# First stage of a transformer layer: its sixteen feature blocks in groups of 3, 4, 4 and 5 in place of 4, 4, 4 and 4

## The chip, the core and the metric

The kernel runs on one core of a Trainium2 chip. Its time is the device time of one execution in microseconds; the time before is the median of three runs. TensorE (PE) multiplies and transposes, VectorE (DVE) and ScalarE (ACT) work on elements, GpSimd (POOL) and SyncE (SP) mostly issue DMA transfers. The clock that TensorE was granted was 0.998 of full speed in the profiled execution.

## The reference

One layer: a first gated feed-forward network, a token mixer, a second gated feed-forward network, each with residual and layer norm. The first stage is all that matters here:

```python
ada = jax.nn.silu(c) @ w_ada + b_ada              # w_ada 2048 x 9*2048
sh1, sc1, g1, sh2, ... = jnp.split(ada, 9)
h = layernorm(x) * (1 + sc1) + sh1                # x: 256 x 2048
gate, up = jnp.split(h @ ffn1_w_in, 2)            # ffn1_w_in 2048 x 2*5632
h = (jax.nn.silu(gate) * up) @ ffn1_w_out
```

All is float32. The 2048 features are 16 blocks of 128. Before TensorE can multiply a block of h, that block's shift and scale must be there, and those are sums over all 2048 rows of two columns of w_ada: 16 rows of 128, each scaled by silu(c) and added on DVE (two operations in one instruction), then transposed by TensorE (which puts features on partitions) and reduced by DVE over the 128 partial sums.

## The kernel before, in words

*Products.* Each product of two float32 matrices is three matmuls of rounded parts: `mm3` multiplies high by high, high by low and low by high (L396, L397, L398). So each weight tile that lands from memory (`raw`) is split: ACT casts it to `hi` (L145), DVE subtracts to get `lo` (L146). The same is done with the activations: `modulate_both` normalises four blocks (L316), transposes them on TensorE (L322), applies shift and scale into the one buffer `xf`, copies it to xhi (ACT, L330) and subtracts to xlo (DVE, L332).

*Passes and tiles.* The first 12 of the column strips of ffn1_w_in (24 chunks of gate and up columns, 6144 columns) are worked in four passes, j = 0 to 3, one for each group of four feature blocks, because the shifts and scales of a later group are not there at the start. A pass has 12 tiles, n = 0 to 11: tile n is a weight tile of 512 rows (4 blocks) by 512 columns, one transfer of 1 MB on SP's queue, 48 matmuls (two halves of 24). Results of passes 0 to 2 are added up in `hT` and `gate` by DVE (L836); the last tile of a pass is kept in PSUM and is the first of the next pass. For that the strips rotate by one a pass (`order_of`): in pass 3, tile n holds strip 9, 10, 11, 0, 1, ..., 8. After pass 3 the remaining columns run with all 16 blocks at once.

*The head.* Everything up to the first matmul: `first_ada` brings 16 rows of ada for blocks 0 to 3 (each 128 x 2 x 512, 512 KB, on SP's queue, some in the places of weight tiles), DVE sums them (L158 the first, L160 the others) into `gate`, and the four blocks then go through transposes (L750) and `modulate_both` one after another, woven with the highs and lows of the first weight tile (`raw_first`, four transfers of 256 KB). `load_bcol` brings all nine vectors of biases (144 rows of 128) and transposes them in the head.

*The stream.* `ada_stream` brings the rows of the next three groups, 48 of 512 KB each, on POOL's queue: row r goes into one of three places that rotate (the tag `araw`), and is summed two steps later by DVE. A place is free again when its row is summed, and POOL, which issues its transfers in order, waits for that. How many steps are taken before a tile is written out by hand: a list of 1s and 2s in pass 0, then `1 + ((n - 11) % 3 == 2)` a tile, 16 a pass. In the middle of tile 10 of a pass, `columns0` transposes the finished sums of the next group (L792) and DVE reduces them (L794); then come four blocks of `modulate_both`, which pass j + 1 needs.

*Pass 3* has no stream any more: from its fourth tile on `pump` brings the ada rows of later stages (`ar2_0_...`, also in the three `araw` places, issued by SP), and DVE sums them between the weight tiles' low parts.

*What sets the order.* DVE and ACT of the last piece of the head run in the order that is written; elsewhere a scheduler arranges each engine's instructions from the program order and dependences, and the order is fixed when the kernel is built. Each engine then works strictly in its order. The pair of buffers `h0` (2 x 128 x 512) is not used by the kernel in the first stage; later stages use it.

Of the kernel before, what the change touches and what calls it, by code (L numbers as in the profile page):

```python
# [47 lines left out]
def layer_kernel(  # L48
# [67 lines left out]
    def load_bcol():  # L116
        brow = ap.tile([72, 2, P], F32, tag="acc", name="brow")
        SP.dma_start(brow, b_ada[0].rearrange("(h r p) -> r h p", h=2, p=P))
        bps = aux_tile("bps")
        for i in range(2):  # L120
            PE.transpose(bps[:, i * 72:(i + 1) * 72], brow[:, i, :], ident[:72, :72])
        V.tensor_copy(bcol.rearrange("p v k -> p (v k)"), bps[:, :144])
        for v in (1, 4, 7):
            V.tensor_scalar_add(bcol[:, v, :], bcol[:, v, :], 1.0)
# [4 lines left out]
    def load_mixer_smalls():  # L129
        hrow = ap.tile([6, 1024], F32, tag="acc", name="hrow")  # L130
        SP.dma_start(hrow[0:4, :], mlstm_conv_w[0])
        SP.dma_start(hrow[4:5, :], mlstm_conv_b)
# [8 lines left out]
        V.tensor_copy(hcol.rearrange("p a b -> p (a b)"), hps[:, :48])
# [170 lines left out]
    def modulate_both(v, j, rs, xT):  # L312
        xf = npool.tile([P, 4, T], F32, tag="xf", name=f"xf{ntag()}")
        n = xf.rearrange("p k t -> p (k t)").rearrange("p (a n) -> p a n", a=2)
        for a in range(2):
            S.activation(n[:, a, :], res[:, a, j * 512:(j + 1) * 512], AF.Identity, bias=rs[a][:, 1:2],  # L316
                         scale=rs[a][:, 0:1])
        yield
        tps = [aux_tile(f"tp{ntag()}") for _ in range(2)]
        for q in range(4):  # L320
# [4 lines left out]
        for q in range(4):  # L325
            k = 4 * j + q
# [3 lines left out]
            high[0] = S.copy(hi, xf[:, q, :])  # L330
            yield
            modulated[0] = V.tensor_tensor(out=lo, in0=xf[:, q, :], in1=hi.bitcast(F32), op=ALU.subtract)  # L332
            yield
# [376 lines left out]
    def first_ada(j, ws=iter(())):  # L710
        src = pair_cols(0, j)
        if j % 2:
            acc = ap.tile([P, 2, 512], F32, tag="acc", name=f"acc0_{j}")
        else:
            acc = gate[:, :1024].rearrange("p (v n) -> p v n", v=2)
        for kk in range(8):
            if kk in (2, 5, 7):
                raws = []
                for h in range(2):
                    k = 2 * kk + h  # L720
                    raw = ap.tile([P, 2, 512], F32, tag="araw", bufs=3, name=f"ar0_{j}_{k}")
# [24 lines left out]
        cps += [mm_tile(f"cq{q}") for q in range(3)]
# [13 lines left out]
        for q in range(4):  # L760
            next(mb)
            if q < 3:
                column(q + 1)
            next(mb)
            fence0.append(next(lows))
            if q:
                next(highs, None)
        yield

    def ada_stream():  # L770
        rows = []
        for r in range(3 * KD + 2):
            if r >= 2:
                with behind(modulated[0]):
                    ada_acc(*rows.pop(0))
            if r < 3 * KD:
# [5 lines left out]
                G_.dma_start(raw, pair_cols(0, j)[k * P:(k + 1) * P])  # L782
                rows.append((sums0[j], raw, k))
            yield

    sums0 = {}
# [25 lines left out]
    def first_in(j, n, i, ws, middle=None):  # L812
# [43 lines left out]
    def first_ws():  # L856
        raw = wp.tile([P, 4, 512], F32, tag="raw", bufs=3, name="raw_first")
        for k in range(4):
# [3 lines left out]
        ws.extend((k, *(p[k // 2][:, k % 2, :] for p in parts)) for k in range(4))  # L862
# [13 lines left out]
    fa = first_ada(0, first_ws())  # L876
# [26 lines left out]
    for j in range(4):  # L903
        for n, i in enumerate(order_of(j)):
# [3 lines left out]
            for _ in range((1, 1, 2, 2, 1, 2, 2, 1, 2, 2, 2)[n] if j == 0 and n < 11 else 1 + ((n - 11) % 3 == 2)):  # L908
# [3 lines left out]
            elif n == 7:  # L912
                mb = modulate_both(0, j + 1, rs0, xT)
# [519 lines left out]
    for j in range(2, 10):  # L1433
# [3 lines left out]
        if j == 7:  # L1437
            need(11)
            mb = modulate_both(6, 2, mr2, xT)
# [84 lines left out]
```

## Time and profile before

| | |
|---|---|
| median of three runs | 1920.01 us (1917.58 to 1920.4) |
| profiled execution, device time | 1918.75 us |
| its span in the profile | 1917.1 us |
| TensorE busy | 1871.8 us, 98% of the span |
| DVE, ACT, POOL busy | 76%, 49%, 3% |
| bytes moved | 510.89 MB, mean 266 GB/s |
| length of the first stage's four passes | about the first 300 us |

In rows of one engine's work the first number is the time from the span's start, the second the duration in us, then engine, line, operation, output and inputs, size, and in brackets how long the engine was idle just before and what released it. In the tables of windows each engine has its busy time with the number of instructions. Names of buffers in the profile are cut at their numbers: `s` is any tile's result in PSUM, `ar` any row of ada, `raw_s`, `hi_s`, `lo_s` any weight tile of the passes.

### The profile page before, as it was taken

Reading aid. Unit: us, or ns where it says so; the run is one execution under the profiler, and the core shown is the slowest. Engines: PE = TensorE matmul, PEld = TensorE weight load, DVE = VectorE, ACT = ScalarE, POOL = GpSimd, SP = SyncE. Lnnn points to the kernel's source line nnn. Section 1 sums busy time; section 2 is a strip of 40 time slices with the busy share of each in tenths; the row PEclk is TensorE's granted clock in tenths of the full one; section 3 lists DMA queues with packets and bytes.
Section 4 is the critical chain, followed back from the end, with each engine's and each line's share of the span. In section 5 each row is a group of like instructions: output and inputs, shape, how many; then the busy total and the mean of one; then the engine's idle time right before and its main releaser. Section 6 shows DMA issues by size and latency. Waiting matters only on the chain.

```text
span 1917.1 us, 32186 instructions
## 1 busy us (share of the span) xinstructions
PE 1871.8 (98%) x13101; PEld 1718.4 (90%) x13101; DVE 1463.5 (76%) x1762; ACT 939.7 (49%) x1310; POOL 58.0 (3%) x93
## 2 busy tenths in 40 slices
PE   3999999999999999999999999999999999999997
PEld 3999999999988888698999886999999999988886
DVE  6899879777778899688887887777775654555786
ACT  5554444444454464745655534465444444444562
POOL 1211000000000000000000000000000000000000
PEclk9999999999999999999999999999999999999999
DMA  9999879999889787489888884998687656755562
GB/s 358 371 330 325 287 231 308 327 306 332 286 319 322 264 304 262 154 307 315 274 277 280 310 295 160 322 317 271 230 269 253 218 183 195 241 190 186 196 198 88
DMA packets 295867, 510.89 MB, mean 266 GB/s; under 512 B 10882, under 2 KB 159010, under 8 KB 294696
## 3 DMA queue, kind: packets, MB, share of 16 engines
q1 hardware_dynamic: 287944, 480.53, 73.9%
q0 software_dynamic: 7776, 28.32, 4.0%
q8 instruction: 102, 1.67, 0.4%
q14 instruction: 45, 0.37, 0.1%
HBM read 506.71 MB, written 2.10 MB: 265 GB/s over the span
## 4 chain that ended last, share of the span: by engine, by line
PE 94%; DVE 2%; DMA 1%; ACT 1%; issue 0%; SPq 0%; POOL 0%; DVEq 0%; POOLq 0%
PE o_f L396 8%; PE gu_f L397 8%; PE gu_f L398 8%; PE o_f L398 8%; PE gu_f L396 8%; PE o_f L397 8%; PE s L396 5%; PE s L398 5%; PE s L397 5%; PE fh L398 2%; PE fh L396 2%; PE fh L397 2%; PE fs L396 1%; PE fs L397 1%; PE fs L398 1%; PE o_mx L398 1%
## 5 line engine op out<-in xcount | busy, mean ns | idle before, releaser
L160 DVE SCALAR_TENSOR_TENSOR acc<-ar,csil,acc 128x1024 f32<-128x1024 f32 x240 | 307.5, 1281 | 31.7 <-DMA ar<-in_w_ada_dram 31.0
L397 PE MATMUL gu_f<-xlo_f,hi_f2i 128*128 128x256 f32 x768 | 212.4, 277 | 0.0
L398 PE MATMUL gu_f<-xhi_f,lo_f2i 128*128 128x256 f32 x768 | 212.3, 276 | 0.0
L396 PE MATMUL gu_f<-xhi_f,hi_f2i 128*128 128x256 f32 x768 | 212.3, 276 | 0.0
L396 PE MATMUL s<-xhi_f,hi_s 128*128 128x256 f32 x752 | 208.6, 277 | 0.0
L398 PE MATMUL s<-xhi_f,lo_s 128*128 128x256 f32 x752 | 208.0, 277 | 0.0
L397 PE MATMUL s<-xlo_f,hi_s 128*128 128x256 f32 x752 | 207.9, 277 | 0.0
L146 DVE TENSOR_TENSOR lo_f2i<-raw_f2i,hi_f2i 128x1024 fp32r<-128x1024 f32 x96 | 117.7, 1226 | 102.8 <-ACT hi_f2i L145 102.8
L396 PE MATMUL gu_f<-xhi_f,hi_f1i 128*128 128x256 f32 x640 | 177.1, 277 | 0.0
L398 PE MATMUL gu_f<-xhi_f,lo_f1i 128*128 128x256 f32 x640 | 177.0, 277 | 0.0
L397 PE MATMUL gu_f<-xlo_f,hi_f1i 128*128 128x256 f32 x640 | 176.9, 276 | 0.0
L145 ACT CAST hi_f2i<-raw_f2i 128x1024 fp32r<-128x1024 f32 x96 | 100.8, 1050 | 138.1 <-PE gu_f L397 126.0
L145 ACT CAST hi_s<-raw_s 128x1024 fp32r<-128x1024 f32 x94 | 98.0, 1054 | 111.0 <-PE s L397 82.0
L397 PEld LDWEIGHTS gu_f<-xlo_f,hi_f2i 128*128 128x128 f32 x768 | 144.2, 188 | 0.1
L396 PEld LDWEIGHTS gu_f<-xhi_f,hi_f2i 128*128 128x128 f32 x768 | 144.2, 188 | 0.1
L398 PEld LDWEIGHTS gu_f<-xhi_f,lo_f2i 128*128 128x128 f32 x768 | 144.2, 188 | 0.0
L397 PEld LDWEIGHTS s<-xlo_f,hi_s 128*128 128x128 f32 x752 | 141.3, 188 | 0.0
L396 PEld LDWEIGHTS s<-xhi_f,hi_s 128*128 128x128 f32 x752 | 141.2, 188 | 0.0
L398 PEld LDWEIGHTS s<-xhi_f,lo_s 128*128 128x128 f32 x752 | 141.2, 188 | 0.0
L145 ACT CAST hi_f1i<-raw_f1i 128x1024 fp32r<-128x1024 f32 x80 | 83.5, 1050 | 115.6 <-PE gu_f L397 75.7
L146 DVE TENSOR_TENSOR lo_f2o<-raw_f2o,hi_f2o 128x1024 fp32r<-128x1024 f32 x86 | 105.3, 1225 | 43.1 <-ACT hi_f2o L145 43.0
L145 ACT CAST hh<-hT 128x512 fp32r<-128x512 f32 x126 | 77.3, 621 | 122.1 <-PE o_f L397 122.0
(503 smaller groups left out, 5436.7 us busy)
## 6 DMA issues: line engine op xcount, KB each, us to landing
ar<-in_w_ada_dram SPq DMA_DIRECT2D x240, 512.0 KB, 6.0
raw_f2i<-in_ffn_w_in_dram SPq DMA_DIRECT2D x48, 1024.0 KB, 5.2
raw_s<-in_ffn_w_in_dram SPq DMA_DIRECT2D x47, 1024.0 KB, 7.6
raw_f1o<-in_ffn_w_out_dram SPq DMA_DIRECT2D x44, 1024.0 KB, 7.3
raw_f2o<-in_ffn_w_out_dram SPq DMA_DIRECT2D x44, 1024.0 KB, 5.2
raw_f1i<-in_ffn_w_in_dram SPq DMA_DIRECT2D x40, 1024.0 KB, 7.5
ar<-in_w_ada_dram POOLq DMA_DIRECT2D x48, 512.0 KB, 7.0
raw_mxo<-in_w_out_dram SPq DMA_DIRECT2D x16, 1024.0 KB, 7.5
```

Source lines behind the costliest of these rows:

```text
L145: S.copy(hi, src)
L146: V.tensor_tensor(out=lo, in0=src, in1=hi.bitcast(F32), op=ALU.subtract)
L160: ins = V.scalar_tensor_tensor(out=acc, in0=raw, scalar=csil[:, k:k + 1], in1=acc, op0=ALU.mult, op1=ALU.add)
L396: PE.matmul(o, ah, bh, start=start, stop=False)
L397: PE.matmul(o, ah, bl, start=False, stop=False)
L398: return PE.matmul(o, al, bh, start=False, stop=stop)
```

## The change

The groups of blocks become `GS = (0, 3, 7, 11, 16)`: pass 0 takes 3 blocks, passes 1 and 2 four each, pass 3 five.

- *Head:* its rows of ada, `raw_first` and the chain through the blocks have three blocks instead of four. Each weight tile of pass 0 is 384 x 512 (0.75 MB) and is split in two parts, of two blocks and of one.
- *Stream:* the 48 rows now bring blocks 3 to 14. Behind them come four units of the columns of block 15, each four rows of 128 x 2 x 128 in one of the `araw` places (pieces of 512 bytes, two transfers), summed by 16 instructions into the first 256 columns of `gate`. The list of steps for pass 0 is kept; then it is `1 + (n % 2 == 0)`, 18 a pass.
- *Block 15:* `last_column` transposes and reduces its sums at the last tile of pass 2, and a `modulate_both` of one block follows the four. In pass 3 each tile has 12 matmuls for it beside the 48: last in the tile's first half, first in its second (`order`). Its weights come on POOL's queue for two tiles at a time, 2 x 256 KB into one `araw` place (`raw_last`, named by the even tile), and `last_w` splits each into the single pair `h0`.
- *Biases:* the head loads the two vectors that the first stage needs (32 rows); the other seven come with `load_mixer_smalls` at the start of pass 3.

The core of the diff:

```diff
-    def load_bcol():
+    def load_bcol(v0, v1, tag):
+        rows = b_ada[0].rearrange("(h r p) -> r h p", h=2, p=P)
+        if v1 == 2:
+            brow = ap.tile([2 * KD, P], F32, tag=tag, name="brow0")
+            SP.dma_start(brow, rows[:2 * KD, 0, :])
...
     def load_mixer_smalls():
+        yield from load_bcol(2, 9, "acc")
...
-    def modulate_both(v, j, rs, xT):
+    def modulate_both(v, k0, nk, rs, xT):
...
+    GS = (0, 3, 7, 11, 16)
+    N0 = GS[1]
+
+    def ada_cols(k0, k1):
+        return w_ada[0, :, :2 * D].rearrange("k (v n) -> k v n", v=2)[:, :, k0 * P:k1 * P]
...
-                    raw = ap.tile([P, 2, 512], F32, tag="araw", bufs=3, name=f"ar0_{j}_{k}")
+                    raw = ap.tile([P, 2, N0 * P], F32, tag="araw", bufs=3, name=f"ar0_0_{k}")
...
     def ada_stream():
         rows = []
-        for r in range(3 * KD + 2):
+        for r in range(3 * KD + 4 + 2):
             if r >= 2:
                 with behind(modulated[0]):
-                    ada_acc(*rows.pop(0))
+                    for add in rows.pop(0):
+                        ada_acc(*add)
...
+            elif r < 3 * KD + 4:
+                u = r - 3 * KD
+                raw = ap.tile([P, 2, 4, P], F32, tag="araw", bufs=3, name=f"ar0_4_{u}")
+                src = ada_cols(15, 16)[u * 512:(u + 1) * 512].rearrange("(k p) v n -> p v k n", p=P)
+                for v in range(2):
+                    G_.dma_start(raw[:, v], src[v])
+                rows.append([(last_sum, raw[:, :, k, :], 4 * u + k) for k in range(4)])
...
+    def last_column():
+        cps = aux_tile("cp4")
+        for v in range(2):
+            PE.transpose(cps[:, v * P:(v + 1) * P], last_sum[:, v, :], ident)
+        cs = scsh[:, 0:2, 15:16]
+        V.tensor_reduce(out=cs, in_=cps[:, :2 * P].rearrange("p (v n) -> p v n", v=2), axis=AX.X, op=ALU.add)
+        V.tensor_tensor(out=cs, in0=cs, in1=bcol[:, 0:2, 15:16], op=ALU.add)
...
     def first_w(j, i):
+        k0 = GS[j]
+        src = W1[k0 * P:min(GS[j + 1], k0 + 4) * P, first_cols(i)]
+        if j == 0:
+            raw = wp.tile([P, N0, 512], F32, tag="raw", bufs=3, name=f"raw_s{j}_{i}")
+            SP.dma_start(raw, src.rearrange("(k p) n -> p k n", p=P))
+            for q in range(0, N0, 2):
+                n = min(2, N0 - q)
+                hi, lo = (wp.tile([P, n, 512], F32R, tag=t, bufs=6, name=f"{t}_s{j}_{i}{q}") for t in ("hi", "lo"))
+                split(raw[:, q:q + n, :], hi, lo)
...
+    def last_w(n, i):
+        if n % 2 == 0:
+            raw = ap.tile([P, 2, 512], F32, tag="araw", bufs=3, name=f"raw_last{n}")
+            for b, ii in enumerate(order_of(3)[n:n + 2]):
+                G_.dma_start(raw[:, b, :], W1[15 * P:, first_cols(ii)])
+                last_raw[ii] = raw[:, b, :]
+        hi, lo = (flat(h) for h in h0)
+        split(last_raw[i], hi, lo)
+        return 15, hi, lo
...
-            for k, hi, lo in ws:
+            if j == 3:
+                x = last_w(n, i) if h == 0 else x
+            order = ws if j < 3 else [x, *ws] if h else [*ws, x]
+            for at_, (k, hi, lo) in enumerate(order):
...
-            for _ in range((1, 1, 2, 2, 1, 2, 2, 1, 2, 2, 2)[n] if j == 0 and n < 11 else 1 + ((n - 11) % 3 == 2)):
+            for _ in range((1, 1, 2, 2, 1, 2, 2, 1, 2, 2, 2)[n] if j == 0 and n < 11 else 1 + (n % 2 == 0)):
...
+                if j == 2:
+                    last_column()
+                    for _ in modulate_both(0, 15, 1, rs0, xT):
+                        pass
```

The order at three places. First, DVE at the end of pass 0, where the next group's last two rows (14 and 15, into `acc0_1`) are summed and its sums reduced (`cp1`, `cq1`). Before:

```order
L146 TENSOR_TENSOR lo_s0_100_933<-raw_s0_10_930,hi_s0_100_932 128x1024
L146 TENSOR_TENSOR lo_s0_101_937<-raw_s0_10_930,hi_s0_101_936 128x1024
L160 SCALAR_TENSOR_TENSOR acc0_1_260<-ar0_1_14_873,csil_94,acc0_1_260 128x1024
L160 SCALAR_TENSOR_TENSOR acc0_1_260<-ar0_1_15_876,csil_94,acc0_1_260 128x1024
L146 TENSOR_TENSOR lo_s0_110_1014<-raw_s0_11_1011,hi_s0_110_1013 128x1024
L146 TENSOR_TENSOR lo_s0_111_1018<-raw_s0_11_1011,hi_s0_111_1017 128x1024
L158 TENSOR_SCALAR gate_104<-ar0_2_0_941,csil_94 128x1024
L146 TENSOR_TENSOR lo_s1_110_1089<-raw_s1_11_1086,hi_s1_110_1088 128x1024
L146 TENSOR_TENSOR lo_s1_111_1093<-raw_s1_11_1086,hi_s1_111_1092 128x1024
L794 TENSOR_REDUCE scsh_103<-cp1_972 128x4
```

The change:

```order
L157 TENSOR_TENSOR lo_s0_100_797<-raw_s0_10_794,hi_s0_100_796 128x1024
L157 TENSOR_TENSOR lo_s0_102_801<-raw_s0_10_794,hi_s0_102_800 128x512
L171 SCALAR_TENSOR_TENSOR acc0_1_244<-ar0_1_14_749,csil_94,acc0_1_244 128x1024
L171 SCALAR_TENSOR_TENSOR acc0_1_244<-ar0_1_15_752,csil_94,acc0_1_244 128x1024
L157 TENSOR_TENSOR lo_s0_110_866<-raw_s0_11_863,hi_s0_110_865 128x1024
L157 TENSOR_TENSOR lo_s0_112_870<-raw_s0_11_863,hi_s0_112_869 128x512
L169 TENSOR_SCALAR gate_104<-ar0_2_0_805,csil_94 128x1024
L157 TENSOR_TENSOR lo_s1_110_929<-raw_s1_11_926,hi_s1_110_928 128x1024
L157 TENSOR_TENSOR lo_s1_111_933<-raw_s1_11_926,hi_s1_111_932 128x1024
L816 TENSOR_REDUCE scsh_103<-cp1_830 128x4
```

Nothing moved: the same order, with the second low part of pass 0's tiles half as large. Second, DVE in pass 3, from tile 7's results to tile 8's low parts (`s3_4` are the results of strip 4, tile 7; `ar2_0_3` is the pump's row 3). Before:

```order
L836 TENSOR_TENSOR hT1_1_109<-hT1_1_109,s3_4_0_3217 128x512
L836 TENSOR_TENSOR hT1_1_109<-hT1_1_109,s3_4_1_3218 128x512
L160 SCALAR_TENSOR_TENSOR acc2_0_2999<-ar2_0_3_3203,csil_94,acc2_0_2999 128x1024
L146 TENSOR_TENSOR lo_s3_70_3410<-raw_s3_7_3407,hi_s3_70_3409 128x1024
L160 SCALAR_TENSOR_TENSOR acc2_0_2999<-ar2_0_4_3205,csil_94,acc2_0_2999 128x1024
L146 TENSOR_TENSOR lo_s3_71_3414<-raw_s3_7_3407,hi_s3_71_3413 128x1024
```

The change:

```order
L899 TENSOR_TENSOR hT1_1_109<-hT1_1_109,s3_4_0_3217 128x512
L899 TENSOR_TENSOR hT1_1_109<-hT1_1_109,s3_4_1_3218 128x512
L171 SCALAR_TENSOR_TENSOR acc2_0_2951<-ar2_0_3_3203,csil_94,acc2_0_2951 128x1024
L157 TENSOR_TENSOR lo_s3_71_3459<-raw_s3_7_3452,hi_s3_71_3458 128x1024
L171 SCALAR_TENSOR_TENSOR acc2_0_2951<-ar2_0_4_3205,csil_94,acc2_0_2951 128x1024
L157 TENSOR_TENSOR h0_1_113<-raw_last8_3299,h0_0_112 128x512 x2
L157 TENSOR_TENSOR lo_s3_80_3543<-raw_s3_8_3540,hi_s3_80_3542 128x1024
```

Two low parts of block 15 (`h0_1` from `raw_last8`, for strips 5 and 6) stand behind row 4, the first low part of strip 7 has moved ahead of tile 7's results. Third, TensorE in the same place of the change, where block 15's matmuls of strip 5 (`s3_5`, from `h0`) come:

```order
L407 MATMUL s3_7_0_3462<-xhi_f1_120,hi_s3_71_3458 128x256
L408 MATMUL s3_7_0_3462<-xlo_f1_121,hi_s3_71_3458 128x256
L407 MATMUL s3_5_0_3297<-xhi_f1_120,h0_0_112 128x256
L408 MATMUL s3_5_0_3297<-xlo_f1_121,h0_0_112 128x256
L407 MATMUL s3_5_1_3298<-xhi_f1_120,h0_0_112 128x256
L408 MATMUL s3_5_1_3298<-xlo_f1_121,h0_0_112 128x256
L409 MATMUL s3_7_0_3462<-xhi_f1_120,lo_s3_71_3459 128x256
L407 MATMUL s3_7_0_3462<-xhi_f1_120,hi_s3_71_3458 128x256
L409 MATMUL s3_5_0_3297<-xhi_f1_120,h0_1_113 128x256
L409 MATMUL s3_5_1_3298<-xhi_f1_120,h0_1_113 128x256
L407 MATMUL s3_5_0_3297<-xhi_f1_120,h0_0_112 128x256
L408 MATMUL s3_5_0_3297<-xlo_f1_121,h0_0_112 128x256
```

Ahead of these rows stand 24 matmuls of strip 5, 24 of strip 6 and 8 of strip 7, all with their own tiles' weights: 56 since tile 7's last. The first with block 15's weights of strip 5 is the third row here.

More of the change, by code (lines that the diff above doesn't have):

```diff
@@ L114, in layer_kernel @@
     G_.memset(mhalf, -0.5)
-    def load_bcol():
[L117 to L122, printed above, removed]
+    def load_bcol(v0, v1, tag):
[3 more added lines that the diff above has]
+            SP.dma_start(brow, rows[:2 * KD, 0, :])
+            parts = [(brow, 2 * KD)]
+        else:
+            brow = ap.tile([72, 2, P], F32, tag=tag, name="brow")
+            SP.dma_start(brow, rows)
+            parts = [(brow[:, i, :], 72) for i in range(2)]
+        yield
+        bps = aux_tile(f"bps{v0}")
+        for i, (part, n) in enumerate(parts):
+            PE.transpose(bps[:, i * 72:i * 72 + n], part, ident[:n, :n])
+        V.tensor_copy(bcol[:, v0:v1, :].rearrange("p v k -> p (v k)"), bps[:, v0 * KD:v1 * KD])
         for v in (1, 4, 7):
-            V.tensor_scalar_add(bcol[:, v, :], bcol[:, v, :], 1.0)
+            if v0 <= v < v1:
+                V.tensor_scalar_add(bcol[:, v, :], bcol[:, v, :], 1.0)
+        yield
     gbias = cst.tile([P, 16], F32, name="gbias")
@@ L324, in modulate_both @@
         yield
-        for q in range(4):
-            k = 4 * j + q
+        for q in range(nk):
+            k = k0 + q
             S.activation(xf[:, q, :], tps[q // 2][:, (q % 2) * T:(q % 2 + 1) * T], AF.Identity,
@@ L759, in first_ada @@
         column(0)
-        for q in range(4):
+        for q in range(N0):
             next(mb)
-            if q < 3:
+            if q < N0 - 1:
                 column(q + 1)
@@ L817, in first_in @@
         hold = n == NS - 1 and j < 3
-        first, last = old is None, 4 * j + 3
+        first = old is None
         ws = list(ws)
@@ L826, in first_in @@
                     mm = mm3(ps[:, h * T:(h + 1) * T], hi[:, fs], lo[:, fs], xT[0][:, k, :], xT[1][:, k, :],
-                             first and h == 0 and k == 4 * j, not hold and h == 1 and k == last)
+                             first and h == 0 and at_ == 0, not hold and h == 1 and at_ == len(order) - 1)
         if hold:
@@ L856, in first_ws @@
     def first_ws():
-        raw = wp.tile([P, 4, 512], F32, tag="raw", bufs=3, name="raw_first")
-        for k in range(4):
+        raw = wp.tile([P, N0, 512], F32, tag="raw", bufs=3, name="raw_first")
+        for k in range(N0):
             SP.dma_start(raw[:, k, :], W1[k * P:(k + 1) * P, :512])
@@ L861, in first_ws @@
                  for t in ("hi", "lo")]
-        ws.extend((k, *(p[k // 2][:, k % 2, :] for p in parts)) for k in range(4))
+        ws.extend((k, *(p[k // 2][:, k % 2, :] for p in parts)) for k in range(N0))
         yield
@@ L1438, in layer_kernel @@
             need(11)
[L1439 removed]
+            mb = modulate_both(6, 8, 4, mr2, xT)
             next(mb)
```

61 lines of the change are left out of this document (33 added, 28 removed).

## The prediction

> **What bounds the kernel now.** I read part 1 of the page first, then the chain of waits, then the first 330 us by windows and engine by engine in order of time, since the change lies there.
>
> ```profile
> span 1917.1 us, 32186 instructions
> PE 1871.8 (98%) x13101; PEld 1718.4 (90%) x13101; DVE 1463.5 (76%) x1762; ACT 939.7 (49%) x1310; POOL 58.0 (3%) x93
> PE 94%; DVE 2%; DMA 1%; ACT 1%; issue 0%; SPq 0%; POOL 0%; DVEq 0%; POOLq 0%
> ```
>
> TensorE sets the end: 98% busy, 94% of the chain. A change gains only where TensorE waits, and every wait that it makes is paid in full. The windows give where it waits in the first stage (from the left: us, PE, PEld, DVE, ACT, POOL, clock, DMA share, GB/s).
>
> ```profile
> 0.00:20.00 20.00, 1.81 (x8) 1.33 (x9) 9.03 (x12) 11.95 (x16) 4.33 (x15) 1.00 0.91 334
> 20.00:34.00 14.00, 2.86 (x13) 2.08 (x11) 12.98 (x15) 1.74 (x4) 2.36 (x3) 1.00 1.05 387
> 34.00:50.00 16.00, 15.58 (x108) 15.28 (x109) 12.96 (x20) 12.28 (x19) 1.45 (x2) 1.00 1.02 368
> 50.00:60.00 10.00, 10.00 (x90) 10.00 (x90) 8.69 (x8) 6.22 (x9) 2.17 (x3) 1.00 1.00 362
> 60.00:70.00 10.00, 10.00 (x91) 10.00 (x90) 7.18 (x7) 5.66 (x8) 2.17 (x3) 1.00 1.03 384
> 70.00:80.00 10.00, 10.00 (x91) 10.00 (x90) 9.96 (x10) 5.93 (x8) 2.89 (x4) 1.00 1.01 373
> 80.00:90.00 10.00, 10.00 (x91) 10.00 (x90) 7.13 (x6) 6.05 (x8) 1.45 (x2) 1.00 1.03 385
> 120.00:140.00 20.00, 20.00 (x179) 20.00 (x178) 18.93 (x21) 8.20 (x8) 4.34 (x6) 1.00 0.96 345
> ```
>
> TensorE idles for 34 us, then never. But the DMA engines are full (share 1.0) until 90 us. Pass 0 feeds TensorE just in time: there is no spare bandwidth under it. A matmul costs 20.00 / 179 = 0.112 us. Five points of TensorE's timeline carry the sum: first matmul, first matmul of the second tile, and the transposes of the next group's sums in passes 0, 1 and 2.
>
> ```profile
> 34.42 0.58 PE L396 MATMUL s<-xhi_f,hi_first 128*128 128x256 f32 x1 [0.54 <-ACT xhi_f L330]
> 43.25 0.28 PE L396 MATMUL s<-xhi_f,hi_s 128*128 128x256 f32 x1
> 95.83 0.60 PE L792 MATMUL cp<-ident,acc 128*128 128x128 f32 x4
> 162.97 0.60 PE L792 MATMUL cp<-ident,gate 128*128 128x128 f32 x4
> 230.11 0.60 PE L792 MATMUL cp<-ident,acc 128*128 128x128 f32 x4
> ```
>
> The last three are 67.14 us apart, twice: passes 1 and 2 run without a wait. The point at 95.83 I call M.
>
> **The change, part by part.**
>
> *Head.* Sixteen ada rows must be summed before the first matmul.
>
> ```profile
> 10.24 0.75 DVE L158 TENSOR_SCALAR gate<-ar,csil 128x1024 f32<-128x1024 f32 x1 [8.06 <-DMA ar<-in_w_ada_dram]
> 18.92 13.54 DVE L160 SCALAR_TENSOR_TENSOR gate<-ar,csil,gate 128x1024 f32<-128x1024 f32 x11
> 26.51 6.32 DMA raw_first<-in_ffn_w_in_dram
> ```
>
> The rows shrink from 1024 columns to 768. DVE: 13.54 / 11 = 1.23 us a row, a quarter off is 0.31, times 16 is 4.9 us. Bytes: 16 x 0.131 = 2.10 MB at 387 GB/s is 5.4 us. They run side by side and the slower one decides; DMA of raw_first stands on the chain too, with a wait that need not shrink. I take 5.2 (bounds 4.3 and 5.9): first matmul at 29.2. In the first tile each block's x is made in a chain that repeats every 1.47 us:
>
> ```profile
> 36.21 0.68 DVE L871 TENSOR_TENSOR lo_first<-raw_first,hi_first 128x512 fp32r<-128x512 f32 x1
> 37.68 0.68 DVE L871 TENSOR_TENSOR lo_first<-raw_first,hi_first 128x512 fp32r<-128x512 f32 x1
> ```
>
> One link (1.47) and six matmuls of the second half (0.67) go: the tile's 8.83 us become 6.69, the second tile starts at 35.9. From there M was 52.58 us away; 114 of 456 matmuls go (12.7 us), so M could come at 75.75, 20.08 earlier. Pass 0 behind M has 18 matmuls fewer (2.0 us), pass 3 has 144 more (16.1 us). **If nothing waits: 20.08 + 2.0 - 16.1 = 6.0 us gained.**
>
> *The stream under pass 0.* It still brings sixteen 512 KB rows for the next group, now under three quarters of the matmuls, and M waits for the sum of its last row.
>
> ```profile
> POOL ar L782 <- DVE acc L160: 30.5, 14, 3.4
> DVE acc L160 <- DMA ar<-in_w_ada_dram: 7.3, 7, 2.1
> 46.56 0.75 DVE L158 TENSOR_SCALAR acc<-ar,csil 128x1024 f32<-128x1024 f32 x1
> 83.22 0.72 POOL L782 DMA_DIRECT2D ar<-in_w_ada_dram  x1 [3.37 <-DVE acc L160]
> 90.34 1.28 DVE L160 SCALAR_TENSOR_TENSOR acc<-ar,csil,acc 128x1024 f32<-128x1024 f32 x1 [0.56 <-DMA ar<-in_w_ada_dram]
> 96.74 0.69 DVE L794 TENSOR_REDUCE scsh<-cp 128x4 f32<-128x512 f32 x1
> 99.61 0.76 DVE L332 TENSOR_TENSOR xlo_f<-xf,xhi_f 128x256 fp32r<-128x256 f32 x2 [1.38 <-ACT xhi_f L330]
> 102.10 0.76 DVE L332 TENSOR_TENSOR xlo_f<-xf,xhi_f 128x256 fp32r<-128x256 f32 x2 [1.74 <-ACT xhi_f L330]
> ```
>
> Before, the last row was summed at 91.62 and TensorE came at 95.83: 4.2 us of slack. The new time is not in the trace; two bounds. *By bytes:* the windows sum to 33.0 MB by 90 us. The change needs 2.10 MB less for the head and 12 x 0.262 = 3.15 less of weights: 27.8 MB. 12.1 are there at 34 us, the other 15.7 at 374 GB/s (mean of the five windows) take 42 us: 75.9, summed at 77.2; at 387, 75.8. *By places:* three places rotate, POOL issues only when DVE frees one, and a row waits 7.1 us (83.22 to 90.34). Sixteen rows took 43.8 us from 46.56. Their first sum moves to about 39 (the second tile's landing moves by 7, then two tiles' low parts, each 0.5 shorter); at the old pace the last is summed at 84.1. Since the windows show full engines, bytes are the nearer row, but DVE sums in order and waits cannot be given back: I take 79.0, 3.25 us behind 75.75 (bounds 0 and 8.35). [...]
>
> *Behind M.* DVE does four low parts and a first multiply between the last sum and the reduce: 96.74 - 91.62 = 5.1 us, hidden before because TensorE came late. Now M follows the sum at once and 0.5 of a smaller low part goes: reduce at M + 4.6, x's first low part 3.2 us and its last 6.1 us after that. TensorE starts pass 1 at M + 1.6 + 6.0 and wants blocks 3 and 4 some 1.4 us on: about 1.0 us lost (0 to 1.5).
>
> *Passes 1 and 2.* Two more rows a pass, 2.6 us of DVE, where the window at 120 leaves 1.07 of 20 idle, 3.6 of 67: nothing, covered by tiles split ahead; with that cover gone up to 2.6. Sixteen quarter sums and 512-byte pieces of ada for block 15 come at the end of pass 2, when no other rows are wanted; up to 2 us if they land late. Two sum transposes and two x transposes of block 15 and the two of the later biases leave the idle head for the busy TensorE: 6 x 0.11 = 0.6. With 0.3 for x of block 15, which waits for the one xf buffer, I put **0.9**.
>
> *Pass 3.* Block 15's split weights have one buffer pair, rewritten in the 5.4 us between two uses: covered. Their raw tiles share the rotation with the pump's rows, and that is not covered at tile 8: its raw tile takes the place of pump row 3, whose sum stands on DVE behind tile 7's adds.
>
> ```profile
> 268.21 1.28 DVE L836 TENSOR_TENSOR hT<-hT,s 128x512 f32<-128x512 f32 x2
> 270.13 0.62 ACT L145 CAST h<-hT 128x512 fp32r<-128x512 f32 x1 [1.72 <-DVE hT L842]
> 272.41 0.69 DVE L146 TENSOR_TENSOR h<-hT,h 128x512 fp32r<-128x512 f32 x1
> ar<-in_w_ada_dram POOLq DMA_DIRECT2D x48, 512.0 KB, 7.0
> gate<-in_b_ada_dram POOLq DMA_DIRECT2D x6, 512.0 KB, 5.4
> raw_first<-in_ffn_w_in_dram SPq DMA_DIRECT2D x4, 256.0 KB, 5.6
> ```
>
> From tile 7's last matmul: adds 1.3, row 1.3, signals 0.5, then a 256 KB transfer on POOL that the trace does not have. Bounds: 4.2 (the quickest stream row) and 7.0; by the 5.4 and 5.6 rows, and a quieter stage, I take 5.0. Cast 0.6: first use at 8.7. The order puts 56 other matmuls first, 6.25 us: TensorE waits 2.5, and 0.3 for the low part. With 0.1 for tile 10: **2.9** (0 to 5.0). Behind the waiting POOL transfer stand only later tiles of this kind; behind the waiting cast, weights that are due a tile later.
>
> *Sum:* -6.0 + 3.25 + 1.0 + 0.9 + 2.9 = **+2.05 us**. The profiled execution took 1918.75 us, 1.65 of it around the span; the median of three is 1920.01, 1.26 above. On the median: **1922.0**.
>
> **The rivals.**
>
> *The stream lands in time.* M at 76 or earlier and block 15's tile within 6.25 us of tile 7's end: -6.0 + 0 + 0.5 + 0.6 + 0.2 = -4.7, 1915.3. For it: 387 GB/s from 20 to 34 us and 385 at 80, when nothing but the engines set the pace. Against: the seven waits of DVE for rows, though the need per us was lower.
>
> *The rows keep their old pace.* Weights and rows split the engines as they do now, 0.524 MB in 2.92 us, whatever the tile size, because SP's queue always holds a tile. Then M is at 84.1, 5.1 us worse than the forecast: +7.2, 1927.2, slower than before. It decides from M = 80.8 on. For it: the pace of 2.92 us held from the first to the last row. Against: by 84 us 31 MB would have flowed, 3 MB more than all that DVE's order lets SP ask for. [...]
>
> *Pass 3 pays more.* With 7.0 us for each late tile it is 2.0 more, 1924: a step inside the forecast's range.
>
> **How the numbers follow.** About 0.2%, 3.8 us, is what a measurement of this kernel tells from no change. Forecast 0.53, its own range 1918 to 1924; stream in time 0.20; old pace 0.27. So faster 0.20, same 0.53, slower 0.27. The range takes in both rivals, the first with half a microsecond less lost behind M: 1914.8 to 1927.5.
>
> **What would show it.** In the changed profile: first matmul near 29.2 and second tile near 35.9 (head); the sums' transposes of pass 0 near 79, not 76 or 84 (stream), with DVE's waits for rows above 7.3 us; the same transposes in passes 1 and 2 still 67 us apart; a wait of TensorE of 2 to 3 us at tile 8 of pass 3 that goes back to ACT's cast of the last block's weights. I am wrong if the head gains under 4 us, if passes 1 or 2 stretch by over 1 us, or if anything beyond the first 340 us moves.

## The result

The change is slower: 1935.09 us (median of four, 1933.53 to 1936.31) against 1919.01 (1917.58 to 1920.40; a fourth run of the kernel before has joined the three behind 1920.01), ratio 1.0084, 95% interval 1.0072 to 1.0097. The forecast was 1922.0 with a range up to 1927.5; the time lies 8 us beyond it. The profiled execution took 1936.31 us.

The page of the change, its span, engines and the chain's shares by engine:

```profile
span 1934.6 us, 32270 instructions
PE 1879.3 (97%) x13102; PEld 1723.2 (89%) x13102; DVE 1467.1 (76%) x1790; ACT 942.7 (49%) x1323; POOL 70.4 (4%) x113
PE 80%; DVE 3%; ACT 1%; DMA 1%; issue 1%; POOL 0%; DVEq 0%; POOLq 0%; ACTq 0%
```

TensorE no longer runs through: its busy time grew by 7.5 us, though the matmuls are the same, and its idle time by 10. The windows of the change say where (columns as in the prediction):

```profile
34.00:50.00 16.00, 16.00 (x143) 16.00 (x142) 11.87 (x13) 9.80 (x15) 2.90 (x4) 1.00 0.97 319
50.00:60.00 10.00, 8.10 (x68) 7.70 (x67) 7.11 (x8) 5.08 (x8) 2.17 (x3) 1.00 0.97 340
70.00:80.00 10.00, 8.35 (x72) 8.02 (x70) 7.62 (x8) 5.08 (x8) 2.17 (x3) 1.00 1.00 353
80.00:90.00 10.00, 7.64 (x64) 7.24 (x63) 8.84 (x12) 6.59 (x12) 2.17 (x3) 1.00 1.01 370
200.00:220.00 20.00, 15.98 (x132) 15.78 (x131) 16.06 (x26) 6.41 (x7) 3.66 (x6) 0.94 0.77 264
220.00:240.00 20.00, 18.17 (x140) 17.95 (x140) 13.66 (x22) 9.41 (x17) 0.54 (x1) 0.89 0.71 244
280.00:300.00 20.00, 17.75 (x152) 17.35 (x151) 15.02 (x18) 6.93 (x9) 1.07 (x2) 0.99 0.74 246
300.00:320.00 20.00, 18.73 (x150) 18.53 (x150) 13.78 (x17) 8.89 (x11) 1.07 (x2) 0.92 0.58 185
```

A full window of 20 us holds 178 or 179 matmuls. There are three places: pass 0 (50 to 90), the end of pass 2 (200 to 240) and the second half of pass 3 (280 to 320). In the last two the granted clock, ahead of the DMA share, also falls below 1. TensorE in order of time, the rows with a wait and the transposes of the sums (`cp`) that mark M in passes 0, 1 and 2:

```profile
29.03 0.80 PE L407 MATMUL s<-xhi_f,hi_first 128*128 128x256 f32 x2 [0.72 <-ACT xhi_f L341]
52.84 0.38 PE L407 MATMUL s<-xhi_f,hi_s 128*128 128x256 f32 x1 [0.49 <-ACT hT L897]
58.65 0.38 PE L407 MATMUL s<-xhi_f,hi_s 128*128 128x256 f32 x1 [1.41 <-ACT hT L897]
77.96 0.39 PE L409 MATMUL s<-xhi_f,lo_s 128*128 128x256 f32 x1 [1.65 <-DVE lo_s L157]
82.25 0.65 PE L814 MATMUL cp<-ident,acc 128*128 128x128 f32 x4 [2.19 <-DVE acc L171]
148.39 0.60 PE L814 MATMUL cp<-ident,gate 128*128 128x128 f32 x4
217.33 0.39 PE L407 MATMUL s<-xhi_f,hi_s 128*128 128x256 f32 x1 [4.02 <-DVE hT L899]
221.45 0.60 PE L814 MATMUL cp<-ident,acc 128*128 128x128 f32 x4
230.71 0.33 PE L333 MATMUL tp<-ident,xf 128*128 128x128 f32 x1 [1.83 <-ACT xf L327]
299.68 0.58 PE L407 MATMUL s<-xhi_f,h 128*128 128x256 f32 x1 [2.09 <-ACT h L156]
314.65 0.39 PE L407 MATMUL s<-xhi_f,h 128*128 128x256 f32 x1 [1.27 <-ACT h L156]
```

Between these points stand the stages. The last one ends at the first matmul of the work behind pass 3 (305.3 us before, 324.0 in the change); from there to the span's end all kernels here take 1610.5 to 1613.3 us, so the whole difference is made before it. Forecast by its own terms; e7, e9 and e10 are experiments below.

| us | before | forecast | change | e10, change again | e7 | e9 |
|---|---|---|---|---|---|---|
| start to first matmul | 34.42 | 29.2 | 29.03 | 28.89 | 28.82 | 28.86 |
| first matmul to M, pass 0 | 61.41 | 49.8 | 53.22 | 57.10 | 54.36 | 46.97 |
| pass 0 to pass 1 | 67.14 | 66.1 | 66.14 | 67.93 | 66.57 | 68.02 |
| pass 1 to pass 2 | 67.14 | 67.1, and 0.9 in all | 73.06 | 68.51 | 67.77 | 67.14 |
| pass 2 to the end of pass 3 | 75.19 | 94.2 | 102.55 | 101.07 | 95.08 | 94.91 |

**What stops TensorE in pass 2.** TensorE waits at 217.33 for DVE's add that empties PSUM. DVE, ACT and POOL just before:

```profile
205.63 1.09 POOL L864 DMA_DIRECT2D raw_last<-in_ffn_w_in_dram  x2 [1.53 <-DVE gate L171]
212.24 0.62 ACT L156 CAST h<-raw_last 128x512 fp32r<-128x512 f32 x1 [9.26 <-DMA raw_last<-in_ffn_w_in_dram]
212.89 0.69 DVE L157 TENSOR_TENSOR h<-raw_last,h 128x512 fp32r<-128x512 f32 x1 [3.69 <-ACT h L156]
216.59 1.28 DVE L899 TENSOR_TENSOR hT<-hT,s 128x512 f32<-128x512 f32 x2
```

It is block 15's first weight tile, `raw_last0`. It needs a place that the ada rows of block 15 hold, so POOL issues it only at 205.63, and it lands 6.6 us later. ACT stands 9.26 us at its cast and DVE 3.69 us at its subtraction. Both engines have work behind it that is due earlier: ACT four casts of the next weight tiles, DVE sums, a low part and the adds. No matmul needs block 15's part before pass 3.

**The clock.** Behind the waits at 217, 230 and 299 TensorE was granted less than full speed for about 4 us. The windows there (engines as above, clock third from the end):

```profile
217.00:219.00 2.00, 1.67 (x9) 1.67 (x10) 2.00 (x4) 0.00 (x0) 0.00 (x0) 0.68 0.60 223
219.00:221.00 2.00, 2.00 (x11) 2.00 (x11) 1.97 (x4) 0.00 (x0) 0.00 (x0) 0.50 0.24 30
231.00:233.00 2.00, 2.00 (x13) 1.97 (x12) 0.87 (x1) 1.57 (x4) 0.00 (x0) 0.60 0.04 7
233.00:235.00 2.00, 2.00 (x12) 2.00 (x11) 1.56 (x2) 0.79 (x3) 0.00 (x0) 0.55 0.92 288
300.00:302.00 2.00, 2.00 (x11) 2.00 (x11) 0.35 (x1) 0.00 (x0) 0.00 (x0) 0.50 1.09 378
302.00:304.00 2.00, 2.00 (x15) 2.00 (x15) 0.49 (x1) 0.62 (x1) 0.00 (x0) 0.73 0.20 76
```

At the full clock such a window shows 19 to 21 matmuls, since those that reach into it are counted. In TensorE's rows the matmuls behind the three waits start 0.213 us apart (218.03, 218.25, 218.46 and so on) in place of 0.112, 15, 17 and 14 times, and 46 x 0.101 = 4.6 us is what the slow clock cost. The waits behind the first matmul sum to 15.3 us of idle time (the eight behind the first matmul in TensorE's rows above, and two of 0.17 us). Each costs some 0.27 more than its row shows: a matmul's row lasts 0.28 us where the next starts 0.112 later, and the first one behind a wait takes 0.38. So 15.3 + 2.7 + 4.6 + 0.6 for transposes - 6.0 (what the forecast gained if nothing waits) = 17.2 of the 18.7 us by which the first stage grew; 1.5 are left that I can't put to a row.

### The profile page after: what moved, and what is told of

Its sections match the earlier page's. It is cut to its first block, busy times and chain, and to the rows that moved or that the text cites. A ratio compares the mean times of both kernels' runs of the same rounds, so it can differ in the third digit from the quotient of the medians.

```text
span 1934.6 us, 32270 instructions
## 1 busy us (share of the span) xinstructions
PE 1879.3 (97%) x13102; PEld 1723.2 (89%) x13102; DVE 1467.1 (76%) x1790; ACT 942.7 (49%) x1323; POOL 70.4 (4%) x113
## 4 chain that ended last, share of the span: by engine, by line
PE 80%; DVE 3%; ACT 1%; DMA 1%; issue 1%; POOL 0%; DVEq 0%; POOLq 0%; ACTq 0%
PE o_f L407 8%; PE gu_f L407 8%; PE gu_f L408 8%; PE o_f L409 8%; PE gu_f L409 8%; PE o_f L408 8%; PE fh L407 2%; PE fh L409 1%; PE fh L408 1%; PE fs L409 1%; PE fs L407 1%; PE fs L408 1%; PE o_mx L409 1%; PE o_mx L407 1%; PE o_mx L408 1%; PE pr_f L409 1%
## 5 line engine op out<-in xcount | busy, mean ns | idle before, releaser
L407 PE MATMUL s<-xhi_f,hi_s 128*128 128x256 f32 x708 | 198.8, 281 | 6.1 <-DVE hT L899 4.0
L409 PE MATMUL s<-xhi_f,lo_s 128*128 128x256 f32 x708 | 197.0, 279 | 1.6 <-DVE lo_s L157 1.6
L408 PE MATMUL s<-xlo_f,hi_s 128*128 128x256 f32 x708 | 197.2, 279 | 0.1
L407 PEld LDWEIGHTS s<-xhi_f,hi_s 128*128 128x128 f32 x708 | 134.8, 190 | 7.0 <-DVE hT L899 4.2
L156 ACT CAST hi_s<-raw_s 128x1024 fp32r<-128x1024 f32 x94 | 91.9, 1001 | 96.7 <-DMA raw_s<-in_ffn_w_in_dram 54.6
L409 PEld LDWEIGHTS s<-xhi_f,lo_s 128*128 128x128 f32 x708 | 134.4, 190 | 1.8 <-DVE lo_s L157 1.8
L408 PEld LDWEIGHTS s<-xlo_f,hi_s 128*128 128x128 f32 x708 | 134.7, 190 | 0.3 <-DVE xlo_f L343 0.3
```

Of the source, the lines that this page charges most:

```text
L156: S.copy(hi, src)
L407: PE.matmul(o, ah, bh, start=start, stop=False)
L408: PE.matmul(o, ah, bl, start=False, stop=False)
L409: return PE.matmul(o, al, bh, start=False, stop=stop)
```

## The experiments

The question was which of the late transfers, the written order and the bytes cost what. e1 to e6 each change one thing of the change; e7 puts two remedies together; e8 is one part of the change alone; e9 closes the sum; e10 is the change again. e1 to e6 were executed once each, and the change's eight executions lie between 1933.53 and 1939.07 us, so a total alone tells little; what counts are the rows.

**e1, half of pass 0's weights.** One transfer serves two tiles, so the weights of every second one are left out:

```diff
-            raw = wp.tile([P, N0, 512], F32, tag="raw", bufs=3, name=f"raw_s{j}_{i}")
-            SP.dma_start(raw, src.rearrange("(k p) n -> p k n", p=P))
+            if i % 2:
+                even[0] = wp.tile([P, N0, 512], F32, tag="raw", bufs=3, name=f"raw_s{j}_{i}")
+                SP.dma_start(even[0], src.rearrange("(k p) n -> p k n", p=P))
+            raw = even[0]
...
```

> The change with less to bring in pass 0: every second weight tile of pass 0 is not loaded, its matmuls and splits use the tile before (so the weights of those strips are left out; all instructions but the transfers stay). 4.7 MB fewer to move before the sums' transposes of pass 0 (M, 82.25 us in the change). Theory bytes (full DMA engines set the pace of the rows): the rows come faster than one in 2.81 us, TensorE's four waits in pass 0 (5.74 us together) go, M at 76 to 77, execution about 1929. Rival places (three places, and DVE summing in its written order, set the pace): the rows keep 2.7 to 2.8 us each, M stays at 81 to 82.5, execution 1934 to 1936.

Measured 1928.25 us. TensorE's waits up to pass 1:

```profile
75.41 0.66 PE L814 MATMUL cp<-ident,acc 128*128 128x128 f32 x4 [0.24 <-DVE acc L171]
84.24 0.39 PE L407 MATMUL s<-xhi_f,hi_s 128*128 128x256 f32 x1 [1.58 <-ACT xhi_f L341]
```

M comes where the forecast's first rival wanted it. The rows come faster with the same three places and nearly the same order on DVE (early in the pass low parts and row sums have changed places), because a row lands 6.0 us after its issue and not 6.9; e6 and e10, with all the weights, have 6.8 and 7.5. So the transport of bytes decides pass 0. The 1.58 us behind M are the x chain that the forecast put at 1.0 (0 to 1.5).

**e2, a fourth place for the rows.**

```diff
...
-        for r in range(3 * KD + 4 + 2):
-            if r >= 2:
+        for r in range(3 * KD + 4 + 3):
+            if r >= 3:
...
+                if r % 4 == 3:
+                    raw = lastp.tile([P, 2, 512], F32, tag="arow", bufs=1, name=f"ar0_{j}_{k}")
+                else:
+                    raw = ap.tile([P, 2, 512], F32, tag="araw", bufs=3, name=f"ar0_{j}_{k}")
...
-            for _ in range((1, 1, 2, 2, 1, 2, 2, 1, 2, 2, 2)[n] if j == 0 and n < 11 else 1 + (n % 2 == 0)):
+            for _ in range((2, 1, 2, 2, 1, 2, 2, 1, 2, 2, 2)[n] if j == 0 and n < 11 else 1 + (n % 2 == 0)):
```

> The change with one more place for the stream's rows (every fourth row in a place of its own, summed three steps later in place of two, and two rows asked for at the first tile). Theory bytes: a fourth row only waits longer in the full engines, M stays within 1 us of 82.25, time from issue to landing grows from 6.9 to over 8 us, execution 1934 to 1936. Rival places: the pace falls from 2.81 to about 2.3 us a row and M comes at 76 to 78, execution about 1930.

Measured 1932.97 us, and neither theory was right alone. TensorE around M, and ACT:

```profile
79.45 0.60 PE L818 MATMUL cp<-ident,acc 128*128 128x128 f32 x4
91.49 0.39 PE L407 MATMUL s<-xhi_f,hi_s 128*128 128x256 f32 x1 [3.46 <-ACT xhi_f L341]
88.20 1.04 ACT L156 CAST hi_s<-raw_s 128x1024 fp32r<-128x1024 f32 x1 [3.30 <-DMA raw_s<-in_ffn_w_in_dram]
```

The rows came earlier: M is 49.1 us behind the first matmul (30.31, since the extra row is asked for in the head), against 53.2, and against 52.4 at best without the fourth place (the table under e10). But behind M ACT waits 3.30 us for a weight tile, with x in its order behind the cast, and TensorE waits 3.46 us. Pass 1's transposes come 121.3 us behind the first matmul, where the change needs 119.4: what the rows gained was lost again at a late weight tile. The windows from 34 to 82 us (busy time of TensorE, clock, DMA share, GB/s), for before, the change, e2 and e1:

```profile
34.00:82.00 48.00, 47.58 (x391) 1.00 1.02 372
```

```profile
34.00:82.00 48.00, 42.51 (x365) 1.00 0.98 341
```

```profile
34.00:82.00 48.00, 46.18 (x396) 1.00 1.00 365
```

```profile
34.00:82.00 48.00, 47.76 (x421) 1.00 0.89 294
```

A pass of three blocks wants 12 tiles of 0.786 MB and 16 rows of 0.524 MB, 17.8 MB, in 12 x 36 x 0.112 = 48.4 us: 368 GB/s. Four blocks want 21.0 MB in 64.5 us: 325 GB/s. The first is about what the engines brought before (372) and more than they brought in the change (341); the second is well below both.

Whether the rows gain what the weights lose is not shown: the weight tiles of pass 0 land 9.4 us after their issue in e2 and 7.2 in the change's first profile, but 9.5 in the change again (e10), which has no fourth place.

**e3, block 15's first split later in DVE's order.**

```diff
...
-        split(last_raw[i], hi, lo)
+        with behind(unit_end[0] if n == 0 else None):
+            split(last_raw[i], hi, lo)
```

> The change, with one thing moved: DVE's split of block 15's first weight tile (raw_last0), which stands among the sums of block 15's ada columns in pass 2, is issued behind the last of these sums. Its transfer is not touched. Theory order (DVE waits 3.69 us there for a late tile, and what is queued behind it, the low parts and the adds that empty PSUM, stops TensorE for 4.02 us): the wait goes, the transposes of passes 1 and 2 are 67.5 us apart in place of 73.06, nothing else moves, execution 1929 to 1930. Rival load (two more rows and sixteen quarter sums are too much for DVE in pass 2): they stay 70 us or more apart, execution 1932 or more.

Measured 1934.88 us. ACT and TensorE:

```profile
212.83 0.62 ACT L156 CAST h<-raw_last 128x512 fp32r<-128x512 f32 x1 [9.60 <-DMA raw_last<-in_ffn_w_in_dram]
216.31 0.39 PE L408 MATMUL s<-xhi_f,hi_s 128*128 128x256 f32 x1 [1.90 <-DVE hT L901]
229.76 0.48 PE L334 MATMUL tp<-ident,xf 128*128 128x128 f32 x1 [2.37 <-ACT xf L328]
```

Some 5 us more than expected. The transposes of passes 1 and 2 are 69.34 us apart and not 67.5; the change itself, run again, has 68.51 (e10), so what the move was worth can't be read from this distance. DVE no longer waits at the split, but ACT still stands 9.60 us at the cast, ahead of four weight casts, and DVE then waits for those. So my theory had the wrong engine: DVE's wait was a consequence, ACT's order the cause, which e5 tests.

**e4, places of their own for block 15's weights.**

```diff
...
-            raw = ap.tile([P, 2, 512], F32, tag="araw", bufs=3, name=f"raw_last{n}")
-            for b, ii in enumerate(order_of(3)[n:n + 2]):
-                G_.dma_start(raw[:, b, :], W1[15 * P:, first_cols(ii)])
-                last_raw[ii] = raw[:, b, :]
+        last_raw[i] = lastp.tile([P, 512], F32, tag="alast", bufs=2, name=f"raw_last{n}")
+        G_.dma_start(last_raw[i], W1[15 * P:, first_cols(i)])
```

> The change with block 15's weights in two places of their own, one 256 KB tile each, in place of sharing the three places of the rows. Theory shared places: the tiles come in time, the waits of TensorE in pass 3 (0.17, 2.09 and 1.27 us) go with the slow clock behind them, and DVE's wait in pass 2 too: about 10 us less, 1924 to 1926. Rival (in pass 3 it is not the tile that is late but the engines' order, casts behind adds): the waits of pass 3 stay, execution 1929 to 1930.

Measured 1932.50 us, 7 more than expected, though the waits named went: pass 3 has none, and that of pass 2 fell from 4.02 to 0.40. The loss is in the head:

```profile
30.83 0.79 PE L407 MATMUL s<-xhi_f,hi_first 128*128 128x256 f32 x2 [0.71 <-ACT xhi_f L341]
86.27 0.66 PE L815 MATMUL cp<-ident,acc 128*128 128x128 f32 x4 [2.88 <-DVE acc L171]
```

With a free place nothing held the first of these transfers back, and the scheduler put it, its cast and its subtraction among the head's rows: the first matmul comes 1.8 us later.

**e5, the same, asked for late.** ACT's cast and DVE's subtraction of the first tile come only behind the four blocks' x:

```diff
...
+        with behind({0: row_dma[3, 12], 1: row_dma[4, 3]}.get(n)):
+            G_.dma_start(last_raw[i], W1[15 * P:, first_cols(i)])
...
+        with behind(four[0] if n == 0 else None):
+            split(last_raw[i], hi, lo)
```

> As e4 (block 15's weights in two places of their own), but the first tile is asked for only behind row 12 of the stream's last group, not in the head where e4 put it ahead of the first matmul, and ACT casts it only behind the four blocks' x (in e3 ACT stood 9.6 us at this cast with four weight casts behind it). Theory: ACT's cast of a late tile, in its order ahead of weights that are due, was the cause of the wait in pass 2, and shared places that of the waits in pass 3. Then the head and pass 0 are those of the change (first matmul 29.0, M 82 to 83), the transposes of passes 1 and 2 are 67.5 us apart, no wait in pass 3, execution 1924 to 1926. Rival (pass 2's stall is also DVE's load of sums): still 69 us or more apart, 1926 to 1928.

Measured 1929.53 us. The head is the change's again (28.87), passes 1 and 2 are 67.14 us apart (151.77 to 218.91), as before the change, and pass 3 has no wait: the mechanism is as expected, and the sums on DVE cost nothing. The time misses by 3.5 to 5.5 us: M came at 85.20 and not at 82 to 83, with the same instructions in the same order up to there, and the work behind pass 3 took 1613.0 us in place of before's 1611.8. Left behind pass 2 is the wait for block 15's x:

```profile
228.61 0.33 PE L333 MATMUL tp<-ident,xf 128*128 128x128 f32 x1 [2.29 <-ACT xf L327]
```

**e6, a place for block 15's x.**

```diff
...
-                    for _ in modulate_both(0, 15, 1, rs0, xT):
+                    for _ in modulate_both(0, 15, 1, rs0, xT, gate[:, 2 * P:4 * P].rearrange("p (k t) -> p k t", k=1)):
```

> The change, with one thing moved: block 15's normalised x (and its x before the split) stands in free columns of gate, not in the one xf buffer that the four blocks' x still occupies. Theory (TensorE's wait of 1.83 us at 230.71 comes from that buffer): this wait and the half clock behind it go, 2.5 to 3 us less, 1932 to 1933; the waits of pass 2 (4.02) and pass 3 (3.5) stay. Rival (the wait comes from ACT's order, the casts of weights ahead of block 15): the wait stays within 0.5 us, 1935.

Measured 1933.17 us. The releaser and the length of the wait have changed:

```profile
225.09 0.44 PE L333 MATMUL tp<-ident,gate 128*128 128x128 f32 x2 [0.83 <-ACT xf L338]
```

From 1.83 to 0.83, and no slow clock behind it; the stretch from pass 2's transposes to the end of pass 3 takes 98.06 us in place of 102.55. What is left waits for ACT's work on the four blocks' x (L338). What the buffer costs is not firm: 1.0 us by this pair, 0.87 between e5 (2.29) and e7 (1.42), which differ in it alone, while e1, with the one buffer, waits only 1.08.

**e7, e5 and e6 together.**

> e5 and e6 together: everything found behind pass 0 taken away, pass 0 left as the change has it. Theory (what is then left is pass 0: 6.9 us lost before M and 1.0 behind it, against the 5.6 us gained by the shorter head): before plus 2 to 3 us, 1921 to 1922, ratio 1.001 to 1.0015. Rival (further losses of five blocks in pass 3, of small pieces or of the clock, that the waits hide): 1924 or more, ratio above 1.0025.

Measured 1927.73 us (1925.31 to 1928.63), ratio 1.0048 (1.0033 to 1.0063): the rival's time, though not by its reasons. Passes 1 to 3 are mended; it is pass 0 that I had put too low, with M 54.36 behind the first matmul where 46.5 (6.69 + 39.85) would be free of waits. Against e6, whose weights of block 15 still share the rows' places, the last stretch falls from 98.06 to 95.08, by 2.98 us. e7 loses some 1.2 more than e6 at block 15's sums and x (waits of 0.29 and 1.42 against 0.83, each with its 0.27), so the late tiles of pass 3 cost about 4.1, which agrees with e6's three waits for them (0.17, 1.73 and 1.18, with 0.27 each: 3.9).

**e8, the biases alone, on the kernel before.**

```diff
-            load_bcol()
+            for _ in load_bcol(0, 2, "acc"):
+                pass
...
     def load_mixer_smalls():
+        yield from load_bcol(2, 9, "acc")
```

> The kernel before with the one part 'biases in two parts' of the change: 32 rows in the head, the other 112 at the start of pass 3. Theory (a transfer of 74 KB fewer and a shorter copy in a head that waits for sums): 0 to 0.4 us less, same as before within 0.1%. Rival (the second part's transposes and copies stand in the way in pass 3): 0.5 to 2 us more.

Measured 1918.67 us (ten runs) against 1918.05 (thirteen), ratio 1.0002 (0.9993 to 1.0012): no difference. In the profile the first matmul comes at 34.14 in place of 34.42 and M at 95.04 in place of 95.83, and pass 3 has no wait.

**e9, e7 with half of pass 0's weights left out** (the diff of e1).

> e7 with e1's omission: every second weight tile of pass 0 is not loaded and the tile before is used in its place (those weights are left out). Theory (behind the mended places only the bytes of pass 0 cost time): M at 75 to 76 as in e1 (75.41), 1.6 us lost behind it, no other wait of a microsecond but that for block 15's x; about 7 us less than e7: 1919 to 1921 where e7 is 1927.7, so level with the kernel before. Rival (pass 0's loss is the order of small pieces or the three places, and e1's gain came from the quieter passes behind): M at 80 or later, 1924 or more.

Measured 1919.33 us (ten runs) against 1918.65, ratio 1.0009 (0.9999 to 1.0018). M and what follows:

```profile
75.83 0.66 PE L815 MATMUL cp<-ident,acc 128*128 128x128 f32 x4 [0.98 <-DVE acc L171]
85.13 0.38 PE L407 MATMUL s<-xhi_f,hi_s 128*128 128x256 f32 x1 [2.04 <-ACT xhi_f L341]
```

8.4 us less than e7. Even a change that had the bytes of pass 0 for nothing and every late tile mended would be level with before. The x chain behind M (68.02 where 65.1 would be free) and the last stretch (94.91 where 75.19 + 16.1 + 0.6 = 91.9) eat the head's gain.

**e10, the change again.**

> The change itself, once more beside the others, for its spread and as the base of the comparisons: 1933 to 1936.5, M within 2 us of 82.25, the waits of passes 2 and 3 in the same places. If TensorE's half clock behind a wait depends on more than the wait's length, waits of the same length show it in one execution and not in another.

Measured 1936.80 us (1933.85 to 1939.07), ratio 1.0094 (1.0079 to 1.0109). M came at 85.99 (within 2 us of 82.25 was expected), behind a wait of 5.56 us, and in pass 2 the wait was 1.05 in place of 4.02, so that pass 2's transposes stand at 222.43, 1 us from the first profile's 221.45. POOL asked for raw_last0 at 208.82, 3.2 us later than in the first profile, while TensorE was 5.5 later by then: what it has waited for in pass 0 it need not wait for again, so the two losses don't add up. Up to M six profiles have the same instructions in the same order (the change twice, e3, e5, e6, e7). In order of the bytes that flowed from 28 to 82 us, M stands behind the first matmul so:

| | e6 | change | e7 | e3 | e5 | e10 |
|---|---|---|---|---|---|---|
| GB/s, 28 to 82 us | 352 | 346 | 345 | 340 | 339 | 334 |
| us from first matmul to M | 52.4 | 53.2 | 54.4 | 54.0 | 56.3 | 57.1 |

## Why the prediction was wrong

The first stage ended 16.7 us later than forecast (324.0 against 307.3). By the table above pass 0 took 3.4 more than forecast, the stretch between the transposes of passes 1 and 2 took 6.0 more, and the stretch behind those 8.4 more; against the last two only 0.9 had been put. Two steps failed: the rate of the stream under pass 0, and the 0.9.

*Direction and rivals.* Slower was given 0.27 and the range ended at 1927.5. The rival "the rows keep their old pace" came nearest in pass 0 (its M was 84.1, measured 82.25 and 85.99), but its 1927.2 held nothing for pass 2.

*Head: right.* First matmul forecast at 29.2, measured at 29.03.

*The stream under pass 0: the mechanism was seen, the size was wrong.* The term was 3.25 us (0 to 8.35); measured 6.5 in the first profile (82.25 against 75.75) and 10.2 in e10. The step that failed is "374 GB/s, the mean of the five windows": the change moved 334 to 352 in six profiles with the same order. The bytes had been counted right. The change (TensorE's busy time, clock, DMA share, GB/s):

```profile
0.00:34.00 34.00, 9.04 (x37) 1.00 0.97 351
34.00:81.00 47.00, 42.51 (x365) 1.00 0.98 341
```

That is 11.9 and 16.0 MB, 28.0 in all by the time the last row was summed (80.91), against 27.8 in the forecast; but the 16.0 took 47 us, where the forecast had 42 for 15.7. The 374 came from windows in which tiles of 1 MB kept the engines full (DMA share 1.00 to 1.03). That three smaller tiles and three rows keep fewer bytes asked for, 3.9 MB at most against 4.7, fits the lower rate, and e2, with 4.5 MB, moved 367; a run that changed only this was not made. Nor do the profiles tell which comes first, TensorE's waits or the lower rate: in e10, with TensorE 5.5 us later, raw_last0 too was asked for 3.2 us later.

*Behind M: the size was right, in part by luck.* 1.0 forecast, 66.14 - (67.14 - 2.0) = 1.0 measured, but the wait for x that was to cause it is only 0.17 us there (at 89.67). Where M is not late the same chain makes TensorE wait 1.58 (e1) and 2.04 us (e9).

*Passes 1 and 2: this step failed.* "0.9" stood against 5.9 us between the transposes of passes 1 and 2, and 3.8 more behind them for x of block 15 (wait 1.83 and its 0.27, slow clock 17 x 0.101 = 1.7). I had costed the sums, the pieces and the transposes, and those cost nothing (e5: 67.14). I had not costed block 15's first weight tile there, because its matmuls are in pass 3. But the scheduler had put its cast and its subtraction into pass 2, ahead of work that was due, and its transfer behind four units that wait for places. All of that could be read from the order of ACT, DVE and POOL. For x of block 15 the one xf buffer was named, with 0.3 for a wait of 1.83.

*Pass 3: the mechanism was right, the size within its bounds.* 2.9 (0 to 5.0) was forecast at tiles 8 and 10; the waits of the change come to 4.3 (0.17, 2.09 and 1.27, with 0.27 each), those of e6 to 3.9. In parts: TensorE waited 2.09 at tile 8 (2.5 forecast) and 1.27 at tile 10 (0.1 forecast). The row sum that frees the place, ACT's cast at tile 8, and POOL's transfer:

```profile
293.23 1.28 DVE L171 SCALAR_TENSOR_TENSOR acc<-ar,csil,acc 128x1024 f32<-128x1024 f32 x1
299.00 0.62 ACT L156 CAST h<-raw_last 128x512 fp32r<-128x512 f32 x1 [5.03 <-DMA raw_last<-in_ffn_w_in_dram]
295.05 1.07 POOL L864 DMA_DIRECT2D raw_last<-in_ffn_w_in_dram  x2 [19.54 <-DVE acc L171]
```

The transfer took about 3.9 us from its issue to the cast, where the forecast had 5.0. Tile 10 was late by the same chain, one pair on.

*The clock: not considered.* 4.6 us in the first profile; in pass 3 alone 14 x 0.101 = 1.4.

*Nothing beyond the first 340 us moved: right*, within 2 us of one execution.

## What to carry to other kernels

Before a group is made smaller to shorten a head, divide the bytes that must land under it by its matmul time: the smaller group raised the need from 325 to 368 GB/s, and the engines brought 334 to 352. When a change brings a late tile into shared places, look in the written order of every engine for where its cast stands, not only for where its matmuls stand: ACT stood 9.3 us at a tile that no matmul needed for another 25 (first use at 237.43). And a place of its own isn't enough, if nothing holds its transfer back: in e4 it went ahead of the head's rows.

## What the runs showed of the hardware

A short wait of TensorE can cost its clock, and whether it does is not a matter of its length alone. In the change a wait of 1.83 us was followed by 4 us at 0.60 and 0.55, and one of 2.09 in pass 3 by 4 us at 0.50 and 0.73. In e10 a wait of 2.40 us at the place of the first was not (clock 1.00 from 234 to 240 us), and neither was one of 2.19 at the place of the second (1.00 from 302 to 310), nor the change's own 2.19 at M (1.00 from 80 to 90). In e4 and e2 too TensorE waits 2.40 us at the first place: behind it the clock is 0.50 from 232 to 234 us in e4, while in e2 the matmuls start 0.11 us apart, as at the full clock. Two windows of e10, behind its wait of 2.40 (ends at 233.27) and behind its wait of 5.56 at M (busy, clock, DMA share, GB/s):

```profile
234.00:236.00 2.00, 2.00 (x19) 1.00 0.26 33
86.00:88.00 2.00, 2.00 (x10) 0.50 0.41 120
```

The rate at which the same transfers ran in the same order differed by 5% between executions (334 to 352 GB/s from 28 to 82 us), and the distance from the first matmul to M by 4.7 us (52.4 to 57.1). The DMA share was 0.95 to 0.99 there, and TensorE waited in pass 0 in all six: little was spare.
